# Written order on four engines, and attention and norms in one step per weight unit: a two-layer trunk on one Trainium2 core

## The chip, the core and the metric

The kernel runs on one core of one Trainium2 chip. The metric is device time in microseconds (us) of one execution; the median of three runs before the change is 2303.36 us (2301.89 to 2307.71). The profile comes from one further execution.

Five engines work side by side: PE (TensorE, matrix products), DVE (VectorE), ACT (ScalarE), POOL (GpSimd) and SP (SyncE, which only starts DMA transfers here). Each has a queue of its own and takes its instructions in the order in which they stand there; semaphores tell one engine when another's result is ready. An instruction that waits holds up all that stand behind it on its engine.

## The reference

256 rows of width 2048 go through two layers, all in float32. Cut to what matters:

```python
# layer 1
u = rms_norm(h, a_norm_g)
q, k, v, fz = split(u @ a_w_in)              # 3 x 2048 columns and 16 gate columns
q, k = rms_norm per head of 128 (a_q_g, a_k_g)
logf = log_sigmoid(fz + a_b_f)
o = softmax(q k^T / sqrt(128) + c_q - c_k, causal) v     # c = cumsum(logf); 16 heads
h = h + o @ a_w_out
h = h + relu(rms_norm(h) @ w1)**2 @ w2       # 2048 -> 8192 -> 2048
# shared keys and values, then layer 2
k, v = split(rms_norm(h, kv_norm_g) @ kv_w); k = rms_norm per head
q = rms_norm per head of (rms_norm(h, b_norm_g) @ b_w_q)
o = softmax(q k^T / sqrt(128) + bias_by_distance, causal by chunks of 64) v
h = h + o @ b_w_out
h = h + relu(rms_norm(h) @ w1)**2 @ w2
```

## The kernel before

**Precision.** Every weight and every activation is split into a rounded part and a rest (`hi`, `lo`), and a product is made of three: hi x hi, hi x lo, lo x hi (lines 305 to 307). The weight split is `issue` (lines 118 to 127): ACT copies the raw piece to `hi` (L125), DVE subtracts (L126).

**Weights.** They come in 768 pieces of 128 x 1024 floats (512 KB, one DMA on SP each, L115), in the order in which they are used. A piece holds two blocks of 128 rows by 512 columns. `fetch` keeps split pieces ready: before the products of piece n are written, the split of piece n+2 is written, and the loads of pieces up to n+5. There are three buffers for split pieces and four for raw ones. So the split of piece n+2 needs the buffer of piece n-1.

**Panels.** A panel is 512 output columns: eight pieces, each followed by 12 matmuls of 512 columns (two row blocks, two halves, three products) into an accumulator pair in PSUM, of which there are two. `panels` (L309) writes, for each piece: fetch, products, then `run_fill`; after the last piece it writes the evacuation. A "woven" stage runs its first two panels at once, piece by piece in turn, so that its input may arrive late; it takes both accumulator pairs.

**Fill.** `fill` is a list of lists of small work items; `run_fill` pops one list after each piece. `add_fill` lays items over the coming pieces. This is how the work between the products is spread: items at index 3 are written after the fourth next piece.

**Turning data.** The output of a panel has rows on the partitions, the next product wants columns there. DVE transposes blocks of 32 (`blocks32`, L176), then `carry` (L182) writes the tile to DRAM by one DMA (L189) and reads it back by four (L195), on SP. Fill lists of `carry`: store at index 0, reads at 2, use at 6.

**Layer 1 attention.** For each of four groups of four heads there is a q, a k and a v panel. `head_norm` (L328) evacuates q and k: ACT squares, DVE sums, POOL takes the power -0.5, DVE scales and transposes, all at the panel's end. `attend` (L399) lays one `softmax` per head on four consecutive pieces from index 6 on, and one `values` per head three pieces after the last. In the first panel `load_x` (L422) also loads the input (sixteen DMAs of 128 KB), scales and splits it and sums its squares by columns (`ColumnStats`, L225). `gates` (L442) makes the forget gates and `decay_bias` their logits. Then come the output projection with `next_x` (L203: add to h, sum squares, transpose, carry, split), four chunks of MLP, the q projection of layer 2, and its four groups of a k and a v panel.

**Order.** The program is written in this order, but a planner in the compiler sorts each engine's instructions by its own estimate of when their inputs will be ready, with the written place as priority. So an instruction can stand on its engine ahead of ones written before it.

Of the kernel before, what the change touches and what calls it, by code (L numbers as in the profile page):

```python
# [31 lines left out]
REL = 384  # L32


@with_exitstack
def trunk(ctx: ExitStack, tc: tile.TileContext, xT, xr, gs, hg, bf, wgate, w_in, w_oa, w1a, w2a,
          w_kv, w_qb, w_ob, w1b, w2b, rel, out):
    nc = tc.nc
    V, S, G, TE = nc.vector, nc.scalar, nc.gpsimd, nc.tensor
# [19 lines left out]
    x0 = wk.tile([P, T], F32, name="xin", tag="wk")  # L59
    nc.sync.dma_start(x0, xT[:, 0, :])  # L60
    gsb = const.tile([P, 5 * KT], F32, name="gsb")
    nc.sync.dma_start(gsb, gs)
# [46 lines left out]
    def load(parts=1):  # L109
        src = units.popleft()  # L110
        raw = wraw.tile([P, UN], F32, name="raw")
        n = UN // parts
        cuts = [slice(i * n, (i + 1) * n) for i in range(parts)]
        for c in cuts:
            nc.sync.dma_start(raw[:, c], src[:, c])  # L115
        raws.append((raw, cuts))
# [49 lines left out]
    def split_turned(t, n, which, into):  # L166
        x = acts.tile([P, 2, GH, T], F32R, name="act")
        y = qkv.tile([P, GH * T], F32, name="z").rearrange("p (k t) -> p k t", k=GH)
        for j in range(GH):
            m = which * KT + GH * n + j  # L170
            S.activation(y[:, j].rearrange("p (b i c) -> p b i c", b=NB, i=4), t[:, j], AF.Copy, scale=gsb[:, m : m + 1])  # L171
        S.activation(x[:, 0], y, AF.Copy)
        V.tensor_tensor(x[:, 1], y, x[:, 0].bitcast(F32), op=ALU.subtract)
        into.extend(x[:, :, j, :] for j in range(GH))

# [6 lines left out]
    def carry(z, dst):  # L182
# [4 lines left out]
        def rows():  # L187
            box.append(dram.tile([P, w], F32, name="turn", tag=f"turn{w}", bufs=4))
            nc.sync.dma_start(box[0], z)  # L189

        def columns():
            s = box[0].rearrange("(i a) f -> a i f", i=4)
            d = dst.rearrange("p (i f) -> p i f", i=4)
            for j in range(4):
                nc.sync.dma_start(d[32 * j : 32 * j + 32], s[:, :, j * n : (j + 1) * n])  # L195

        return [[rows], [], [columns], [], [], []]
# [5 lines left out]
    def next_x(n, r2, stats, which, into, kept=None):  # L203
# [3 lines left out]
        def use(flipped=False, which=which, into=into):  # L207
# [3 lines left out]
            split_turned(t, n, which, into)  # L211
# [12 lines left out]

    class ColumnStats:  # L225
        def __init__(self):
            self.acc = const.tile([P, T], F32, name="sqacc")
            self.n = 0

        def add(self, x):  # L230
            if self.n == 0:
                S.activation(self.acc, x, AF.Square)
            else:
                t = wk.tile([P, T], F32, name="sqt", tag="wk")
                S.activation(t, x, AF.Square)
                V.tensor_tensor(self.acc, self.acc, t, op=ALU.add)
            self.n += 1

        def reduce(self):
            pm = ps_o.tile([P, 512], F32, name="pt", tag="po")  # L240
            for b in range(NB):
                TE.matmul(pm[:, 2 * b : 2 * b + 2], self.acc[:, b * P : (b + 1) * P], ones[:, :2], start=True, stop=True)
            ms = sm.tile([P, NB], F32, name="ms")
            V.tensor_scalar(ms, pm[:, 0 : 2 * NB : 2], 1.0 / D, EPS, op0=ALU.mult, op1=ALU.add)
            self.r, self.e = root(ms, "a"), scaled(ms, "a")

        def spread(self):
            self.R = const.tile([P, T], F32, name="R")
            pr = ps_o.tile([P, 512], F32, name="pt", tag="po")
            for b in range(NB):  # L250
                rb = wk.tile([P, P], F32, name="rb", tag="wk")
                V.tensor_scalar(rb, ones[:, :P], self.r[:, b : b + 1], None, op0=ALU.mult)
                TE.matmul(pr[:, b * P : (b + 1) * P], rb, ident, start=True, stop=True)
            V.tensor_copy(self.R, pr[:, :T])
# [11 lines left out]
    class RowStats:  # L266
# [22 lines left out]

        def flip(self):  # L290
# [37 lines left out]
    def head_norm(e, z, dst):  # L328
        def f(b, ps):
# [5 lines left out]
            V.tensor_scalar(vv, ss, 1.0 / P, e[:, b : b + 1], op0=ALU.mult, op1=ALU.add)  # L335
# [3 lines left out]
            V.tensor_tensor(qn.rearrange("p (a d) -> p a d", a=GH), ps.rearrange("p (a d) -> p a d", a=GH),  # L339
                            rn.unsqueeze(2).to_broadcast([P, GH, P]), op=ALU.mult)  # L340
            blocks32(qn, z, b)
            if b == NB - 1:
                add_fill(carry(z, dst))
# [17 lines left out]
    def softmax(st, g, a, q, k, bias, cq):  # L361
        s = ps_s.tile([P, 512], F32, name="s")
        TE.matmul(s[:, 0:P], q[:, a, 0:P], k[:, a, 0], start=True, stop=True)
        TE.matmul(s[:, P : 3 * P], q[:, a, P:T], k[:, a], start=True, stop=True)
        t = wk.tile([P, 3 * P], F32, name="t", tag="wk")
# [4 lines left out]
        for b, c in ((0, slice(0, P)), (1, slice(P, 3 * P))):  # L370
# [5 lines left out]
            V.tensor_reduce(nm[:, b : b + 1], t[:, c], axis=AX.X, op=ALU.max, negate=True)  # L376
            S.activation(pr[:, c], t[:, c], AF.Exp, bias=nm[:, b : b + 1], accum_out=su[:, b : b + 1])  # L377
        V.reciprocal(rs, su)
        for b, c in ((0, slice(0, P)), (1, slice(P, 3 * P))):
            V.tensor_scalar(pr[:, c], pr[:, c], rs[:, b : b + 1], None, op0=ALU.mult)  # L380
        st["p"] = pr
        flip(st)

    def flip(st):
        z = prob.tile([P, 3 * P], F32, name="z", bufs=3)
        blocks32(st["p"], z, 0)
        st["pT"] = prob.tile([P, 3 * P], F32, name="prT")
        add_fill(carry(z, st["pT"]))
# [10 lines left out]
    def attend(g, q, k, v, bias, cq, o):  # L399
        st = [{} for _ in range(GH)]  # L400
        k4 = k.rearrange("p (i a b c) -> p a b i c", i=4, a=GH, b=NB)
# [17 lines left out]
    st0 = ColumnStats()  # L419
    x = []  # L420

    def load_x(u):  # L422
        for m in range(u * UA, (u + 1) * UA):
            xm = x0
            if m:
                xm = wk.tile([P, T], F32, name="xin", tag="wk")
                nc.sync.dma_start(xm, xT[:, m, :])
            x.append(split_x(xm, m, 0))
            st0.add(xm)
            if m in (0, UA):  # L430
                issue(2)
        if u == 1:
            nc.sync.dma_start(hgb, hg)
            nc.sync.dma_start(bfb, bf)
            V.tensor_scalar(gqk, hgb[:, 0:2], float(P) ** -0.5, None, op0=ALU.mult)
            V.tensor_tensor(gqk, gqk, hgb[:, 2:4], op=ALU.mult)
        if u == KT // UA - 1:
            st0.reduce()
# [3 lines left out]
    def gates(x, st):  # L442
        wgr = const.tile([P, KT * H], F32, name="wgr")
        nc.sync.dma_start(wgr, wgate)
# [19 lines left out]
        def logs():  # L464
# [8 lines left out]
            V.scalar_tensor_tensor(z, u, -1.0, u, op0=ALU.mult, op1=ALU.max)  # L473
            S.activation(z, z, AF.Exp, scale=-1.0)
            S.activation(z, z, AF.Ln, bias=1.0)
            V.scalar_tensor_tensor(z, u, 0.0, z, op0=ALU.min, op1=ALU.subtract)
            V.tensor_tensor_scan(c, ones[:H, :], z, 0.0, op0=ALU.mult, op1=ALU.add)
            nct = wk.tile([H, REL], F32, name="nct", tag="wk")
# [3 lines left out]
            nc.sync.dma_start(ct["cd"], nct)  # L482
# [8 lines left out]
        return [[lambda u=u: products(u)] for u in range(KT // UG)] + [[logs], [], [], [], [], [turn_c]]  # L491

    def decay_bias(g):
        nb = qkv.tile([P, GH, REL], F32, name="bias")
        src = ct["cd"][g * GH : (g + 1) * GH, :]
        nc.sync.dma_start(nb, src.unsqueeze(0).to_broadcast([P, GH, REL]))
        for c in (slice(0, P), slice(2 * P, 3 * P)):
            V.tensor_tensor(nb[:, :, c], nb[:, :, c], tri.unsqueeze(1).to_broadcast([P, GH, P]), op=ALU.add)
        return nb

    o = [None] * H
    for g in range(NG):
        zq, lq = turned("z")
        box = {}
        panels(x, [lambda b, ps: head_norm(st0.e, zq, lq)(b, ps)], load_x if g == 0 else None)
        add_fill([[]] * 6 + [[lambda box=box, lq=lq: box.update(q=scale_q(lq, 0))]])
        if g == 0:
            add_fill([[], [], [], [st0.spread]] + gates(x, st0))
        if g == 1:
            for b in range(NB):  # L510
# [3 lines left out]
        panels(x, [head_norm(st0.e, zk, k)])  # L514
        add_fill([[]] * (4 if g == 0 else 0) + [[lambda g=g, box=box: box.update(b=decay_bias(g))]])
        add_fill([[]] * (3 if g == 0 else 0) + attend(g, lambda box=box: box["q"], k, v, lambda box=box: box["b"], lambda: ct["cq"], o))
        panels(x, [v_evac(v, st0.r)])

    def mlp(x, st, last):
        for c in range(NCH):  # L520
            hid = []

            def take(t):
# [4 lines left out]
                S.activation(hi, t, AF.Square)  # L528
                S.activation(t, t, AF.Square)  # L529
                V.tensor_tensor(lo, t, hi.bitcast(F32), op=ALU.subtract)  # L530
                hid.extend(y[:, :, j, :] for j in range(GH))

            def turn_hidden():
                zt = []

                def f(b, ps):
# [3 lines left out]
                    if b == NB - 1:  # L540
                        add_fill(carry(*zt) + [[lambda: take(zt[1])]])
# [11 lines left out]
    add_fill([[], [st2.both], [st2.flip], []] + [[lambda n=n: kept[n](True, 2, xkv)] for n in range(NG)])  # L553
# [3 lines left out]
    for g in range(NG):  # L557
        box = {}

        def f(b, ps, box=box):  # L560
            if b == 0:
                z, lq = turned("z")
                box["f"] = head_norm(st2.e, z, lq)
                add_fill([[]] * 6 + [[lambda: qs.append(scale_q(lq, 1))]])
            box["f"](b, ps)
        evs.append(f)
# [3 lines left out]
    def rel_bias(g):  # L570
# [83 lines left out]
```

## Time and profile before

| what | value |
|---|---|
| median of three runs | 2303.36 us |
| the profiled execution's own time | 2303.8 us |
| its span, first to last instruction | 2301.7 us |
| mean granted TensorE clock | 0.978 |
| weight splits, L125 on ACT and L126 on DVE | 770 each, 1056 and 1218 ns |
| products, L305 to L307 | 3072 each |
| DMA | 491.60 MB, mean 214 GB/s |

The 40 slices of the span show where TensorE is busy and at which clock:

```profile
PE   7989989999999999999998988899999999999999
PEclk8999999999999999999999999999999999999999
DMA  5656666777667667667776755667775775776775
```

Each digit is a fortieth of the span, 57.5 us, in tenths of busy time, of full clock, or of the DMA engines. Layer 1's attention lies in slices 1 to 7, its MLP up to about slice 20, layer 2's attention around slices 22 to 27. A busy TensorE is not one at its peak, as the ends of its records are modelled; the number of matmuls in a window says more. The SP queue's waits, longest first, from its own view:

```profile
SPq L115 <- DVE lo L126: 1416.7, 624, 10.9
SPq L195 <- DMA turn<-z: 110.7, 58, 4.0
SPq L189 <- DVE z L179: 88.8, 63, 4.1
```

That is the line that waits, whom it waits for, the sum in us, how often, and the longest.

### The profile page before, as it was taken

The page shows a single profiled execution, that of the slowest core. Times are in us where ns is not written, and L with a number is a line of the kernel's source. Part 1 is how long each engine was busy: PE and PEld are TensorE (multiplying, and loading weights), DVE is VectorE, ACT ScalarE, POOL GpSimd, SP SyncE. Part 2 cuts the span into 40 slices and gives each one's busy share as a digit, 9 for nine tenths or more (in the row PEclk, how much of TensorE's full clock was granted, in tenths as well). Part 3 has the DMA queues.
Part 4 walks back from the last instruction along what each step waited for, and adds up shares of the span by engine and source line. Part 5 has one row for each costly group of instructions (what it writes and reads, how often), then busy time and mean ns, then how long its engine had stood idle before and what let it go on. Part 6 is the DMA issues. An engine that isn't in the chain of part 4 may idle for free. (4 is left out here: it accounts for less than half of the span.)

```text
span 2301.7 us, 25837 instructions
## 1 busy us (share of the span) xinstructions
PE 2199.6 (96%) x9518; PEld 1802.2 (78%) x9518; DVE 1267.9 (55%) x1478; ACT 1050.0 (46%) x1251; POOL 47.6 (2%) x48
## 2 busy tenths in 40 slices
PE   7989989999999999999998988899999999999999
PEld 4767777787888888888786877777788888888887
DVE  4666555555555555555565655565555555555554
ACT  4443433545345345345564533345543443443443
POOL 0100000000000000000001100000000000000000
PEclk8999999999999999999999999999999999999999
DMA  5656666777667667667776755667775775776775
GB/s 199 217 181 207 222 186 208 239 233 236 197 218 240 194 218 241 195 213 247 207 234 208 226 181 183 188 203 233 221 239 193 231 231 194 229 229 193 228 232 168
DMA packets 184174, 491.60 MB, mean 214 GB/s; under 512 B 36960, under 2 KB 76016, under 8 KB 183792
## 3 DMA queue, kind: packets, MB, share of 16 engines
q1 hardware_dynamic: 184048, 489.96, 67.4%
q8 instruction: 74, 1.21, 0.2%
q14 instruction: 52, 0.43, 0.1%
HBM read 450.01 MB, written 39.87 MB: 213 GB/s over the span
## 5 line engine op out<-in xcount | busy, mean ns | idle before, releaser
L126 DVE TENSOR_TENSOR lo<-raw,hi 128x1024 fp32r<-128x1024 f32 (+1 forms) x770 | 935.5, 1218 | 793.8 <-ACT hi L125 785.8
L125 ACT ACTIVATE hi<-raw 128x1024 fp32r<-128x1024 f32 (+1 forms) x770 | 811.0, 1056 | 990.2 <-PE acc L307 937.3
L305 PE MATMUL acc<-hi,act 128*128 128x512 f32 x3072 | 1216.8, 396 | 47.7 <-ACT hi L125 29.4
L306 PE MATMUL acc<-lo,act 128*128 128x512 f32 x3072 | 1216.5, 396 | 44.4 <-DVE lo L126 44.1
L307 PE MATMUL acc<-hi,act 128*128 128x512 f32 x3072 | 1211.7, 395 | 2.0 <-DVE act L163 1.9
L306 PEld LDWEIGHTS acc<-lo,act 128*128 128x128 f32 x3072 | 585.9, 191 | 177.6 <-DVE lo L126 56.6
L305 PEld LDWEIGHTS acc<-hi,act 128*128 128x128 f32 x3072 | 585.4, 191 | 177.8 <-ACT hi L125 34.9
L307 PEld LDWEIGHTS acc<-hi,act 128*128 128x128 f32 x3072 | 586.5, 191 | 126.3 <-DVE act L163 4.6
L396 ACT ACTIVATE act<-po 128x256 fp32r<-128x256 f32 x32 | 12.3, 384 | 117.5 <-PE po L394 117.5
L397 DVE TENSOR_TENSOR act<-po,act 128x256 fp32r<-128x256 f32 x32 | 13.5, 422 | 87.2 <-ACT act L396 87.2
L179 DVE STREAM_TRANSPOSE z<-acc 128x512 f32<-128x512 f32 x64 | 42.0, 695 | 20.7 <-PE acc L307 20.7
L337 POOL TENSOR_TENSOR rn<-vv,mhalf 128x4 f32<-128x4 f32 x32 | 42.0, 1312 | 440.3 <-DVE vv L335 440.3
L331 ACT ACTIVATE sq<-acc 128x512 f32<-128x512 f32 x32 | 19.0, 598 | 68.7 <-DVE qn L339 33.6
L377 ACT ACTIVATE pr<-t,nm 128x128 f32<-128x128 f32 x64 | 28.7, 449 | 26.3 <-DVE nm L376 25.7
L339 DVE TENSOR_TENSOR qn<-acc,rn 128x512 f32<-128x512 f32 x32 | 22.1, 691 | 32.4 <-POOL rn L337 32.4
L530 DVE TENSOR_TENSOR act<-q,act 128x1024 fp32r<-128x1024 f32 x32 | 39.0, 1218 | 0.0
L333 DVE TENSOR_REDUCE ss<-sq 128x4 f32<-128x512 f32 x32 | 21.6, 674 | 26.5 <-ACT sq L331 26.4
L528 ACT ACTIVATE act<-q 128x1024 fp32r<-128x1024 f32 x32 | 34.0, 1062 | 1.0
L524 ACT ACTIVATE q<-q 128x1024 f32<-128x1024 f32 x32 | 33.4, 1044 | 0.6 <-DMA q<-turn 0.6
L529 ACT ACTIVATE q<-q 128x1024 f32<-128x1024 f32 x32 | 33.3, 1042 | 0.0
L171 ACT ACTIVATE z<-q,gsb 128x256 f32<-128x256 f32 x64 | 27.4, 495 | 3.2 <-DMA q<-turn 2.2
L358 DVE SCALAR_TENSOR_TENSOR h<-acc,qn,h 128x512 f32<-128x512 f32 x32 | 22.6, 747 | 11.0 <-PE acc L307 11.0
(99 smaller groups left out, 432.6 us busy)
## 6 DMA issues: line engine op xcount, KB each, us to landing
raw<-in_w1a SPq DMA_DIRECT2D x128, 512.0 KB, 4.3
raw<-in_w2a SPq DMA_DIRECT2D x128, 512.0 KB, 4.3
raw<-in_w1b SPq DMA_DIRECT2D x128, 512.0 KB, 3.8
raw<-in_w2b SPq DMA_DIRECT2D x128, 512.0 KB, 3.6
raw<-in_w_in SPq DMA_DIRECT2D x94, 512.0 KB, 4.5
raw<-in_w_kv SPq DMA_DIRECT2D x64, 512.0 KB, 4.7
turn<-z SPq DMA_DIRECT2D x60, 512.0 KB, 4.1
q<-turn SPq DMA_DIRECT2D x176, 128.0 KB, 5.5
```

The source lines that it names most:

```text
L125: S.activation(hi[:, c], raw[:, c], AF.Copy)
L126: V.tensor_tensor(lo[:, c], raw[:, c], hi[:, c].bitcast(F32), op=ALU.subtract)
L179: V.transpose(z.rearrange("p (j n b c) -> p b n j c", j=4, n=n, b=nb)[:, b], src.rearrange("p (n j c) -> p n j c", n=n, j=4))
L305: TE.matmul(ps[b], xh, wh, start=k == 0, stop=False)
L306: TE.matmul(ps[b], xh, wl, start=False, stop=False)
L307: TE.matmul(ps[b], xl, wh, start=False, stop=k == KT - 1)
L337: G.tensor_tensor(rn, vv, mhalf, op=ALU.pow)
L377: S.activation(pr[:, c], t[:, c], AF.Exp, bias=nm[:, b : b + 1], accum_out=su[:, b : b + 1])
L524: S.activation(t, t, AF.Relu)
L528: S.activation(hi, t, AF.Square)
L529: S.activation(t, t, AF.Square)
L530: V.tensor_tensor(lo, t, hi.bitcast(F32), op=ALU.subtract)
```

## The change

1. **Order.** At the end of the program `keep_order` adds an ordering edge from each instruction on DVE, ACT, PE and SP to the one written before it on that engine. The planner can then no longer sort these four queues; POOL's is left free.
2. **Attention and norms in steps.** Work items become generators; each `yield` ends what is written after one piece. A head's softmax is four steps (scores; bias and maximum; exponential; normalise and transpose), heads start `GAP` = 3 pieces apart (2 in the last group of a layer), and values follow eight pieces after the scores were begun. `head_norm` keeps its sums at the panel's end, but the scaling and the transpose of each row block are laid on the next two pieces. `next_x` lays its transposes on the next piece, and starts its carry from there. Splits of turned inputs, the MLP's `take`, the gates' `logs`, and the biases are cut in two or three steps. `carry` waits one piece fewer before use, and for attention's probabilities one fewer between store and reads.
3. **Square sums from rows.** `ColumnStats` goes. The first norm's statistics come from `RowStats` on h, whose eight blocks of 256 KB are loaded in pieces 2 to 5 of the first panel and squared in pieces 4 to 7; before, h was loaded by two DMAs of 1 MB, written after the first group.
4. **Input in pairs.** x comes by eight DMAs of 256 KB, two pieces ahead; weight loads in the first panel keep fewer split pieces ready at first.

```diff
+def keep_order(tc, engines):
+
+    last = {}
+    for i in tc.nc.cur_bb.bb.instructions:
+        if i.engine in engines:
+            if i.engine in last:
+                tc.add_manual_dep(i, last[i.engine], mybir.DependencyInfo(mybir.DependencyClass.NoSync, mybir.DependencyReason.DATA),
+                                  reason="written order")
+            last[i.engine] = i.name
...
+    def steps(make):
+        box = []
+
+        def step():
+            if not box:
+                box.append(make())
+            next(box[0])
+        return step
...
-        return [[rows], [], [columns], [], [], []]
+        return [[rows]] + [[]] * wait + [[columns], [], []]
...
+        def turn():
+            zt.extend(turned(bufs=4))
+            for b in range(NB):
+                blocks32(h[b][:, n * 512 : (n + 1) * 512], zt[0], b)
+
         def f(b, ps):
             add_h(b, ps)
             stats.add(b, n)
-            if b == 0:
-                zt.extend(turned(bufs=4))
-            blocks32(h[b][:, n * 512 : (n + 1) * 512], zt[0], b)
             if b == NB - 1:
-                add_fill(carry(*zt) + [[use]])
+                step = steps(use)
+                add_fill([[turn], [lambda: add_fill(carry(*zt) + [[step], [step]])]])
...
-                hi, lo = fetch(min(u, AHEAD), min(u // 2, EARLY)) if before else fetch()
+                hi, lo = fetch(min(u // 2, AHEAD), 2) if before else fetch()
...
-            qn = wk.tile([P, 512], F32, name="qn", tag="wk")
-            V.tensor_tensor(qn.rearrange("p (a d) -> p a d", a=GH), ps.rearrange("p (a d) -> p a d", a=GH),
-                            rn.unsqueeze(2).to_broadcast([P, GH, P]), op=ALU.mult)
-            blocks32(qn, z, b)
+
+            def turn():
+                qn = wk.tile([P, 512], F32, name="qn", tag="wk")
+                V.tensor_tensor(qn.rearrange("p (a d) -> p a d", a=GH), ps.rearrange("p (a d) -> p a d", a=GH),
+                                rn.unsqueeze(2).to_broadcast([P, GH, P]), op=ALU.mult)
+                blocks32(qn, z, b)
+
+            rns.append(turn)
             if b == NB - 1:
-                add_fill(carry(z, dst))
+                add_fill([[t] for t in rns] + carry(z, dst))
...
-        A = [[lambda a=a: softmax(st[a], g, a, q(), k4, bias(), cq() if cq else None)] for a in range(GH)]
-        C = [[lambda a=a: values(st[a], a, v, o, g * GH + a)] for a in range(GH)]
-        return [[]] * 6 + A + [[]] * 3 + C
+        items = [[] for _ in range(15 + gap * GH)]
+        step = steps(lambda: make_bias(g, box))
+        items[1].append(step)
+        items[4].append(step)
+        items[5].append(step)
+        for a in range(GH):
+            at = 7 + gap * a
+            step = steps(lambda a=a: softmax(st[a], g, a, q(), k4, box["b"], cq() if cq else None))
+            for i in range(4):
+                items[at + i].append(step)
+            items[at + 3].append(lambda a=a: add_fill(st[a]["carry"]))
+            items[at + 8].append(lambda a=a: values(st[a], a, v, o, g * GH + a))
+        return items
...
+    def begin(u):
+        if u == 0:
+            load(2)
+            load_x(1)
+            load(2)
+        if u + 2 < KT // UA:
+            load_x(u + 2)
+        for j in range(UA):
+            x.append(split_x(raw_x[u][:, j], u * UA + j, 0))
...
+        if 2 <= u < 6:
+            for b, n in chunks[2 * u - 4 : 2 * u - 2]:
+                c = slice(n * 512, (n + 1) * 512)
+                SY.dma_start(h[b][:, c], xr[b][:, c])
+        if 4 <= u:
+            for b, n in chunks[2 * u - 8 : 2 * u - 6]:
+                st0.add(b, n)
...
-            add_fill([[], [], [], [st0.spread]] + gates(x, st0))
-        if g == 1:
-            for b in range(NB):
-                nc.sync.dma_start(h[b], xr[b])
+            add_fill([[st0.spread]] + gates(x, st0))
...
-    add_fill([[], [st2.both], [st2.flip], []] + [[lambda n=n: kept[n](True, 2, xkv)] for n in range(NG)])
+    again = [steps(lambda n=n: kept[n](True, 2, xkv)) for n in range(NG)]
+    add_fill([[], [st2.both], [], [st2.flip]] + [[]] * 6 + [[again[i // 2]] for i in range(2 * NG)])
...
     mlp(x3, st3, store)
+    keep_order(tc, (V.engine, S.engine, TE.engine, SY.engine))
```

More of the change, by code (lines that the diff above doesn't have):

```diff
@@ L114, in load @@
         for c in cuts:
-            nc.sync.dma_start(raw[:, c], src[:, c])
+            SY.dma_start(raw[:, c], src[:, c])
         raws.append((raw, cuts))
@@ L180, in blocks32, with carry @@
                     src.rearrange("p (n j c) -> p n j c", n=n, j=4))
-    def carry(z, dst):
+    def carry(z, dst, wait=1):
         w = z.shape[1]
@@ L210, in use @@
                 t = t[:, :, :, ::-1, ::-1]
-            split_turned(t, n, which, into)
+            return split_turned(t, n, which, into)
+        def turn():
+            zt.extend(turned(bufs=4))
+            for b in range(NB):
+                blocks32(h[b][:, n * 512 : (n + 1) * 512], zt[0], b)
         def f(b, ps):
@@ L223, in next_x @@
         return f
[L225 to L240, printed above, removed]
-            for b in range(NB):
[L242 to L254, printed above, removed]
     def root(ms, name):
@@ L288, in both, with roots, spread @@
             self.e = scaled(self.ms, self.name)
+        def roots(self):
+            self.both()
+            self.r = root(self.ms, self.name)
+        def spread(self):
+            self.R = const.tile([P, T], F32, name="R")
+            pr = ps_o.tile([P, 512], F32, name="pt", tag="po")
+            for b in range(NB):
+                rb = wk.tile([P, P], F32, name="rb", tag="wk")
+                V.tensor_scalar(rb, ones[:, :P], self.r[:, b : b + 1], None, op0=ALU.mult)
+                TE.matmul(pr[:, b * P : (b + 1) * P], rb, ident, start=True, stop=True)
+            V.tensor_copy(self.R, pr[:, :T])
         def flip(self):
@@ L326, in stage, with head_norm @@
             panels(x, [e])
-    def head_norm(e, z, dst):
+    def head_norm(stats, z, dst):
+        rns = []
         def f(b, ps):
@@ L369, in softmax @@
         rs = sm.tile([P, NB], F32, name="rs")
-        for b, c in ((0, slice(0, P)), (1, slice(P, 3 * P))):
+        halves = ((0, slice(0, P)), (1, slice(P, 3 * P)))
+        for b, c in halves:
             if cq is not None:
@@ L416, in add_fill @@
                 fill.append(it)
-    st0 = ColumnStats()
+    st0 = RowStats("x")
     x = []
[L422 to L431, printed above, removed]
+    chunks = [(b, n) for n in range(NG) for b in range(NB)]
+    def begin(u):
[7 more added lines that the diff above has]
+            x.append(split_x(raw_x[u][:, j], u * UA + j, 0))
         if u == 1:
-            nc.sync.dma_start(hgb, hg)
-            nc.sync.dma_start(bfb, bf)
+            SY.dma_start(hgb, hg)
+            SY.dma_start(bfb, bf)
             V.tensor_scalar(gqk, hgb[:, 0:2], float(P) ** -0.5, None, op0=ALU.mult)
             V.tensor_tensor(gqk, gqk, hgb[:, 2:4], op=ALU.mult)
+        if 2 <= u < 6:
[5 more added lines that the diff above has]
+                st0.add(b, n)
         if u == KT // UA - 1:
-            st0.reduce()
+            st0.roots()
     ct = {}
@@ L481, in logs @@
             ct["cd"] = dram.tile([H, REL], F32, name="cd")
[L482 removed]
+            SY.dma_start(ct["cd"], nct)
+            yield
         def turn_c():
@@ L489, in turn_c, with decay_bias @@
             V.tensor_copy(ct["cq"].rearrange("p b h -> p (b h)"), pc[:, : NB * H])
-        return [[lambda u=u: products(u)] for u in range(KT // UG)] + [[logs], [], [], [], [], [turn_c]]
-    def decay_bias(g):
+        step = steps(logs)
+        return ([[lambda: SY.dma_start(wgr, wgate)], []] + [[lambda u=u: products(u)] for u in range(KT // UG)]
+                + [[step], [step], [step], [], [turn_c]])
+    def decay_bias(g, box):
         nb = qkv.tile([P, GH, REL], F32, name="bias")
         src = ct["cd"][g * GH : (g + 1) * GH, :]
[L496 to L499, printed above, removed]
+        SY.dma_start(nb, src.unsqueeze(0).to_broadcast([P, GH, REL]))
+        yield
+        V.tensor_tensor(nb[:, :, :P], nb[:, :, :P], tri.unsqueeze(1).to_broadcast([P, GH, P]), op=ALU.add)
+        yield
+        c = slice(2 * P, 3 * P)
+        V.tensor_tensor(nb[:, :, c], nb[:, :, c], tri.unsqueeze(1).to_broadcast([P, GH, P]), op=ALU.add)
+        box["b"] = nb
+        yield
     o = [None] * H
@@ L540, in f @@
                     if b == NB - 1:
-                        add_fill(carry(*zt) + [[lambda: take(zt[1])]])
+                        step = steps(lambda: take(zt[1]))
+                        add_fill(carry(*zt) + [[step], [step]])
                 return f
@@ L581, in trunk @@
         v = qkv.tile([P, NB, 512], F32, name="v")
-        panels(xkv, [head_norm(st2f.e, zk, k)])
-        box = {}
-        box["b"] = rel_bias(g)
-        add_fill(attend(g, lambda g=g: qs[g], k, v, lambda box=box: box["b"], None, o))
-        panels(xkv, [v_evac(v, st2f.r)])
+        panels(xkv, [head_norm(lambda: st2.flipped, zk, k)])
+        add_fill(attend(g, lambda g=g: qs[g], k, v, None, o, rel_bias, GAP if g < NG - 1 else 2))
+        panels(xkv, [v_evac(v, st2.flipped.r)])
     st3, x3 = RowStats("n"), []
```

71 lines of the change are left out of this document (43 added, 28 removed).

## The prediction

> **What bounds the kernel now.** I read the page first, then the waits of TensorE, then busy time by stage, then the timeline around one wait.
>
> ```profile
> PE 2199.6 (96%) x9518; PEld 1802.2 (78%) x9518; DVE 1267.9 (55%) x1478; ACT 1050.0 (46%) x1251; POOL 47.6 (2%) x48
> ```
> ```profile
> engine line waited for: us in total, times, longest us
> PE acc L306 <- DVE lo L126: 44.1, 29, 3.6
> PE acc L305 <- ACT hi L125: 29.4, 20, 2.7
> PE acc L305 <- ACT act L162: 11.7, 6, 2.9
> PE acc L305 <- DVE qn L339: 6.4, 1, 6.4
> ```
> TensorE is the bound. DVE and ACT are half idle, yet TensorE waits about 96 us for them, nearly always for a weight split (`hi`, `lo`).
>
> ```profile
> 5.50:54.40 48.90, 33.70 (x97) 22.15 (x97) 21.38 (x41) 19.99 (x38) 0.00 (x0) 0.79 0.61 211
> 54.40:107.70 53.30, 51.33 (x220) 40.96 (x220) 35.12 (x56) 24.09 (x32) 8.55 (x7) 0.97 0.62 201
> 107.70:415.80 308.10, 278.78 (x1185) 225.55 (x1184) 178.93 (x293) 127.91 (x196) 16.89 (x14) 0.96 0.65 204
> 415.80:464.70 48.90, 45.43 (x193) 37.08 (x192) 28.52 (x29) 26.91 (x39) 0.00 (x0) 0.97 0.76 235
> 464.70:1120.10 655.40, 653.11 (x2881) 540.48 (x2881) 352.34 (x323) 305.12 (x301) 0.00 (x0) 1.00 0.69 220
> ...
> 1168.80:1268.00 99.20, 90.37 (x388) 73.73 (x388) 60.46 (x70) 53.61 (x70) 8.61 (x7) 0.97 0.68 212
> 1268.00:1548.60 280.60, 255.30 (x1089) 207.97 (x1088) 159.45 (x270) 116.62 (x183) 12.46 (x12) 0.95 0.63 195
> ```
> The columns are window, its length, busy time of PE, PEld, DVE, ACT and POOL, granted clock, DMA share and GB/s. I call the 12 products of one 128x1024 weight piece a unit; there are 768. The fifth row (240 units, one wait of 2.3) gives the pace: 653.1 / 240 = 2.72 us a unit. Against it: first panel 48.9 - 8 x 2.72 = **27.1 over**. Layer 1's attention to the middle of its output projection (third row, 88 units): 239.4, plus 32 score and value steps of four matmuls at 0.72 us (23.0), leaves **45.7 over**, of which the waits in that window are 29.4. Layer 2's (last row, 80 units): 217.6 + 23.0, **40.0 over**, waits 25.3. So 54.7 us of waits drag 31.0 us of slow clock behind them: 0.57 us for each us waited.
>
> ```profile
> 145.93 0.38 ACT L396 ACTIVATE act<-po 128x256 fp32r<-128x256 f32 x1 [5.22 <-PE po L394]
> 146.22 1.05 ACT L125 ACTIVATE hi<-raw 128x1024 fp32r<-128x1024 f32 x1
> 146.35 0.42 DVE L397 TENSOR_TENSOR act<-po,act 128x256 fp32r<-128x256 f32 x1 [3.96 <-ACT act L396]
> 147.30 1.22 DVE L126 TENSOR_TENSOR lo<-raw,hi 128x1024 fp32r<-128x1024 f32 x1 [0.52 <-ACT hi L125]
> 147.32 0.49 PE L305 MATMUL acc<-hi,act 128*128 128x512 f32 x1 [1.42 <-ACT hi L125]
> ...
> 148.57 0.79 PE L306 MATMUL acc<-lo,act 128*128 128x512 f32 x1 [0.76 <-DVE lo L126]
> ```
> This is the mechanism. ACT stood 5.22 us before a copy that needed this unit's value product, with the next weight split queued behind it. The planner had put L396 ahead of L125, so TensorE waited 1.42 for `hi`, 0.76 for `lo`, and then ran at 0.79 us a matmul record.
>
> [...]
>
> **The change, part by part.** Everything below is in us.
>
> *Written order.* Now `hi` and `lo` of unit n+2 stand on ACT and DVE ahead of the fill items of unit n. They may start when TensorE ends unit n-1, so they have two units, 5.44, for 1.06 + 1.22: TensorE feels nothing until DVE or ACT is 3.16 late. DVE has 2.72 - 1.22 = 1.50 spare a unit, ACT 2.72 - 1.06 = 1.66; a unit with a score or value step gives 0.72 more.
>
> *Attention in steps.* Per head: scores; a unit later DVE adds bias and reduces (0.34 + 0.47 + 0.27 + 0.41 = 1.49); then ACT exp (0.40 + 0.50 + 2 x 0.19 = 1.28); then DVE reciprocal, scaling and transpose (0.16 + 0.28 + 0.35 + 0.57 = 1.36); value step five units on (DVE 0.42). Heads follow three units apart. Head norm leaves 1.8 at a panel's end and moves 0.69 + 0.71 = 1.40 into each of two later units. The worst units, counted from the V panel, are 15 (1.8 + 0.42), 16 (1.36 + 1.40) and 17 (1.49 + 1.40). Backlog after each: 2.22 - 2.22 = 0; 2.76 - 2.22 = 0.54; 0.54 + 2.89 - 1.50 = 1.93; in unit 18 it is gone. 1.93 is under 3.16. Layer 2, sixteen units a group, meets the same sum. The last group's heads two units apart reach 1.35. Each step's input was made a unit earlier, so nothing waits on its neighbour. A transpose issues one row DMA and four column DMAs on SP: rows land in 4.1 (192 KB: 2.5), columns in 5.5; they have 2 (heads: 1) and about 3 units. A load of unit n+5 is needed three units, 8.2, later and lands in 4.5, so SP can stand 3.7 without harm. The cover for all these zeros is that two-unit lead; without it each DVE step costs its 1.4. I leave one 0.76 wait (the `lo` row above) in each of eight groups, with slow clock 8 x 0.76 x 1.57 = 9.5. Bounds: 0, and half of the present overrun, 43. **Gain 85.7 - 9.5 = 76.2.**
>
> *First panel.* x comes in eight 256 KB pairs two units ahead; square sums move to rows of h, whose eight 256 KB loads now stand on SP between x and weights in units 2 to 5. To the last input of the panel SP asks for 8 x 0.26 + 8 x 0.26 + 8 x 0.52 MB = 8.3 MB. The 10 to 25 us windows moved 338 to 371 GB/s: 25 us. So DMA isn't last; ACT is: units 5 to 7 need two splits (0.50), two squares with sums (0.62 + 0.19) and `hi`, 3.68 against 2.72, and unit 4 a second `hi`, 4.74: 3 x 0.96 + 2.0 = 4.9. In unit 1 DVE stands in `gqk` for `hgb` (twelfth on SP, at 0.43 an issue near 5.5; 4.1 to land, behind 2.6 MB), ahead of `lo`: PE idle about 2.7. Together 7.6 x 1.57 = 11.9 over. Bounds: 6, and 22 if DMA stays at this window's 211 GB/s. The dropped column sums (15 DVE adds of 0.42) lay beside idle DVE. **Gain 27.1 - 11.9 = 15.2.**
>
> *Spread and gates.* Written order puts the spread matmuls between units 8 and 9, while their DVE input stands behind both head-norm sums, a `lo` and the first moved step: 2.4 + 1.2 + 1.4 + 0.3 = 5.3 after unit 7, 2.6 late. Each of two gate products waits for POOL's memset (which needs a buffer that the preceding unit frees), ACT and DVE: 0.95 + 0.31 + 0.29 and handover = 1.75, with TensorE standing. 6.1 x 1.57 = 9.6, where the second row above has 53.3 - 43.5 - 4.5 (gate and spread matmuls) = 5.3. **Loss 4.3** (0 to 10).
>
> *Stage seams.* At the end of the first layer's output projection, third panel, DVE ran residual, transposes, then `lo`: 48.9 - 43.5 = 5.4 over; so at three places, 16. Now two residual panels' splits and squares meet in units 22 to 24: `hi` of unit 26 stands behind 3.0 of splits and 1.6 of squares and lets TensorE wait 0.5, `lo` of unit 27 behind a split and the transposes 1.9; 2.4 x 1.57 x 3 = 11.3. **Gain 4.7.** The wait of 2.3 after each first w1 stage goes (DVE has `lo` ahead of the transposes): **gain 4.6.** In layer 2's query stage (99.2 - 87.1 = 12.1 over) the third panel wants the accumulator that the second moved norm step still reads. That step stands behind the kv split, the first step, the second panel's sums and a `lo`: 1.2 + 1.4 + 1.8 + 1.2 + 1.4, and some 1.6 of waiting in front, so TensorE idles about 8.6, x 1.57 = 13.5. **Loss 1.4** (bounds: gain 6, loss 8).
>
> *Sum:* 76.2 + 15.2 - 4.3 + 4.7 + 4.6 - 1.4 = 95.0. The profiled run took 2303.8 with a span of 2301.7; the median is 2303.4, so the same difference is taken from it: **2208**. The MLP units (512 of 768) gain nothing else.
>
> **Rivals.** (a) *All waits go*, the clock never drops in the attention stages, and seams vanish: 2303.4 - 85.7 - 18 - 20 - 5 = 2175. For it: 1.93 against 3.16. Against: DMA landings spread (4.3 median, 10.0 longest for transposes). (b) *Half stays*: columns land late, TensorE now stands in a score or value step where the planner had put it later. 2208 + 43 - 9.5 = 2242. For: k lands about a unit ahead of its first use. Against: values come five units after their weights. (c) *The weight queue becomes the bound*, and the kernel slower. SP in written order holds weight loads behind column DMAs that wait for rows. Once the stand exceeds 3.7 each us reaches TensorE; with 56 transposes in the attention stages it eats the gain from 3.7 + 95 / (56 x 1.57) = 4.8 us a transpose. At 5.5 (the columns' landing) it costs 56 x 1.8 x 1.57 = 158: 2366. For: SP stood 110.7 in 58 such waits. Against: 35.5 of them fell in the 655 us of MLP where TensorE waited 2.3 in all. (d) *The order isn't kept*: the planner still sorts, only the first panel gains: 2288 to 2305, about 2295. (e) *The clock holds through short waits*: the 0.57 parts of my sums fall away, 3.4 + 4.3 + 3.5 + 4.1 + 4.9 = 20.2, so 2188. Against: the 0.79 row above. [...]
>
> **How the numbers follow.** Forecast 0.57, by itself 2185 to 2235; (e) 0.05; (a) 0.10; (b) 0.14; (d) 0.04; (c) 0.10. 0.3% is 7 us, what a measurement of this kernel can tell. Faster: the forecast, (e), (a), (b) and half of (d), 0.88; same 0.02; slower 0.10. The range 2175 to 2260 holds the forecast, (e), most of (b) and a third of (a), about 0.78.
>
> **What would show it.** L396 and L397 after the next L125 and L126; TensorE waits in the attention stages down from 54.7 to some 6; a first panel of 31 to 37 us; short waits at the spread and gate products; one wait near 8 in layer 2's query stage; MLP windows at clock 1.00 and 2.72 a unit. Wrong would be: weight loads as releasers of L125, or many waits of TensorE before L363 or L393.

## The result, and the profile after

The changed kernel takes 2199.97 us (median of four runs, 2196.73 to 2203.54) against 2305.53 (median of four) for the kernel before: ratio 0.9542, 95% interval 0.9519 to 0.9566. Its profiled execution took 2199.56 us with a span of 2197.8. The span is 103.9 us shorter. The page's line on busy time, share and count of each engine:

```profile
PE 2160.6 (98%) x9514; PEld 1781.1 (81%) x9514; DVE 1274.4 (58%) x1464; ACT 1049.1 (48%) x1251; POOL 48.3 (2%) x48
```

The waits of TensorE after the change (line that waits, whom for, sum in us, how often, longest). L142 and L143 are the weight splits, formerly L125 and L126; L319 to L321 are the products.

```profile
PE acc L320 <- DVE lo L143: 7.7, 11, 2.2
PE acc L319 <- DVE qn L357: 7.4, 1, 7.4
PE acc L319 <- ACT hi L142: 7.2, 7, 2.0
PE s L499 <- DVE hi L496: 3.5, 2, 1.7
PE pt L301 <- DVE rb L300: 3.3, 1, 3.3
```

The two waits for weight splits fell from 73.5 to 14.9 us. What is new stands in the last two lines: the gate products (L499) and the spread (L301). By stage, with the columns of the windows shown before (length, PE, PEld, DVE, ACT, POOL, clock, DMA share, GB/s):

```profile
6.60:35.20 28.60, 24.96 (x96) 18.72 (x97) 18.41 (x31) 20.64 (x41) 0.71 (x1) 1.00 0.95 344
35.20:94.20 59.00, 52.23 (x218) 41.96 (x217) 33.85 (x50) 23.23 (x29) 6.65 (x6) 0.94 0.60 194
94.20:356.00 261.80, 261.40 (x1183) 216.77 (x1182) 181.62 (x287) 127.48 (x196) 16.25 (x12) 1.00 0.72 234
...
1108.60:1205.50 96.90, 89.21 (x387) 73.15 (x386) 61.56 (x71) 55.72 (x73) 8.80 (x7) 0.96 0.68 216
1205.50:1445.10 239.60, 239.60 (x1090) 199.28 (x1090) 163.67 (x269) 114.97 (x183) 14.77 (x14) 1.00 0.74 233
```

The third and the last row are the attention stages: clock 1.00, TensorE busy throughout. One wait of 0.4 us is left there, for a probability tile that a DMA brings; it was 54.7. The second row is the place that became worse, at clock 0.94. The table cuts both kernels at the same products. "Over" is what a stage takes beyond 2.72 us for each of its units; the gain is the difference of the stages' times.

| stage | over, before | over, after | gain | forecast |
|---|---|---|---|---|
| first panel (gain includes its start, at 5.5, then 6.6) | 27.1 | 6.9 | 19.1 | 15.2 |
| spread and gates (next two panels) | 9.8 | 15.5 | -5.7 | -4.3 |
| two attention stages, with 46 us of matmuls of their own | 131.7 | 44.2 | 87.5 | 76.2 |
| three residual seams | 16.0 | 19.4 | -3.4 | 4.7 |
| after the first w1 stage of each layer | 5.2 | 1.0 | 4.2 | 4.6 |
| layer 2's query stage | 12.1 | 9.9 | 2.2 | -1.4 |
| sum | | | 103.9 | 95.0 |

A value step of the same group of heads as in the prediction's timeline, now on ACT:

```profile
145.78 0.39 ACT L418 ACTIVATE act<-po 128x256 fp32r<-128x256 f32 x1 [1.34 <-PE po L416]
146.06 1.05 ACT L142 ACTIVATE hi<-raw 128x1024 fp32r<-128x1024 f32 x1
```

In the prediction's timeline ACT stood 5.22 us ahead of such a copy, with a split behind it that TensorE needed next. Now it stands 1.34, and the split behind it isn't needed for two units.

### The profile page after: what moved, and what is told of

Same layout as the page of the kernel before. It is cut to its first block, busy times and chain, and to the rows that moved or that the text cites. A ratio compares the mean times of both kernels' runs of the same rounds, so it can differ in the third digit from the quotient of the medians.

```text
span 2197.8 us, 25786 instructions
## 1 busy us (share of the span) xinstructions
PE 2160.6 (98%) x9514; PEld 1781.1 (81%) x9514; DVE 1274.4 (58%) x1464; ACT 1049.1 (48%) x1251; POOL 48.3 (2%) x48
## 4 chain that ended last, share of the span: by engine, by line
PE 91%; DMA 3%; ACT 2%; DVE 2%; issue 1%; SPq 0%; POOL 0%; DVEq 0%; ACTq 0%; POOLq 0%
PE acc L320 30%; PE acc L321 30%; PE acc L319 30%; DMA raw<-in_w_in 1%; ACT hi L142 1%; DMA turn<-z 1%; DVE lo L143 1%; PE po L415 1%; PE s L384 1%; DMA raw<-in_w_ob 0%; DMA raw<-in_w_oa 0%; ACT act L191 0%; DMA raw<-in_w2a 0%; ACT z L188 0%; PE po L416 0%
## 5 line engine op out<-in xcount | busy, mean ns | idle before, releaser
L143 DVE TENSOR_TENSOR lo<-raw,hi 128x1024 fp32r<-128x1024 f32 (+1 forms) x770 | 936.7, 1218 | 810.5 <-ACT hi L142 802.9
L142 ACT ACTIVATE hi<-raw 128x1024 fp32r<-128x1024 f32 (+1 forms) x770 | 811.7, 1057 | 1002.9 <-PE acc L321 960.5
L319 PE MATMUL acc<-hi,act 128*128 128x512 f32 x3072 | 1210.1, 394 | 15.3 <-DVE qn L357 7.4
L320 PE MATMUL acc<-lo,act 128*128 128x512 f32 x3072 | 1201.1, 391 | 7.7 <-DVE lo L143 7.7
L321 PE MATMUL acc<-hi,act 128*128 128x512 f32 x3072 | 1199.7, 391 | 0.8 <-DVE act L180 0.8
L319 PEld LDWEIGHTS acc<-hi,act 128*128 128x128 f32 x3072 | 579.3, 189 | 137.8 <-ACT hi L142 10.0
L320 PEld LDWEIGHTS acc<-lo,act 128*128 128x128 f32 x3072 | 579.3, 189 | 133.1 <-DVE lo L143 14.5
L321 PEld LDWEIGHTS acc<-hi,act 128*128 128x128 f32 x3072 | 578.8, 188 | 122.6 <-DVE act L180 2.0
L274 ACT ACTIVATE sqr<-h 128x512 f32<-128x512 f32 x32 | 19.9, 624 | 22.3 <-DVE h L376 14.0
L349 DVE TENSOR_REDUCE ss<-sq 128x4 f32<-128x512 f32 x32 | 21.8, 681 | 14.2 <-ACT sq L347 14.2
L192 DVE TENSOR_TENSOR act<-z,act 128x1024 fp32r<-128x1024 f32 x16 | 19.6, 1226 | 10.4 <-ACT act L191 10.4
```

Source lines behind the costliest of these rows:

```text
L142: S.activation(hi[:, c], raw[:, c], AF.Copy)
L143: V.tensor_tensor(lo[:, c], raw[:, c], hi[:, c].bitcast(F32), op=ALU.subtract)
L319: TE.matmul(ps[b], xh, wh, start=k == 0, stop=False)
L320: TE.matmul(ps[b], xh, wl, start=False, stop=False)
L321: TE.matmul(ps[b], xl, wh, start=False, stop=k == KT - 1)
```

## The experiments

Three kernels' worth of change stand in one diff: an order, smaller items, another start. The first runs take the order apart.

**The steps without any order.**

```diff
-    keep_order(tc, (V.engine, S.engine, TE.engine, SY.engine))
```

> The changed kernel without its written order: the planner sorts all queues again, steps and front as changed. Theory (the order took the waits away, the steps only make an order possible that has no long item in it): the planner again puts copies that need a fresh score or value product ahead of weight splits; TensorE waits in the two attention stages for L142/L143 stay at 25 to 50 us (after: 0.4; before: 54.7), time 2235 to 2290. Rival (the small steps alone do it): waits under 5, time 2195 to 2212.

2217.48 us, ratio 0.9607 (0.9579 to 0.9634): neither range. The steps and the new start alone bring 88 of the 106 us. By the spans, 56 us of this lie in the attention stages and 23 in the first panel and its start. In the two attention stages TensorE waits 19 us, 9.0 and 10.0 (here and below, waits of over 0.25 us are added up). The first two rows of its waits over the whole run:

```profile
PE acc L320 <- DVE lo L143: 20.7, 22, 2.3
PE acc L319 <- ACT hi L142: 11.2, 12, 1.9
```

**The order without the steps**, on the kernel before.

```diff
     mlp(x3, st3, store)
+    keep_order(tc, (nc.vector.engine, nc.scalar.engine, nc.tensor.engine, nc.sync.engine))
```

> The kernel before, with the written order on DVE, ACT, PE and SP and nothing else of the change. Theory (order without steps moves the wait): a head's softmax is then one item on four units in a row, DVE 1.49 + 1.36 plus about 0.7 of standing for ACT's exponential, against 1.50 spare, so about 1.3 to 2 late a head, 3.16 of lead per group: some 6 us of waits in each of 8 groups, 48 against 54.7 before; time 2265 to 2320. Rival (the order alone does it): waits under 10, time 2200 to 2230.

2310.34 us, ratio 1.0017 (1.0001 to 1.0032), in the theory's range. Its attention waits are 58.5, where the theory had 48; its first panel is 14 us better than before, and its spread and gates 15 worse.

```profile
PE acc L317 <- DVE lo L137: 77.5, 43, 4.3
PE acc L316 <- ACT hi L136: 8.2, 15, 1.5
```

Where the planner let TensorE wait for ACT and DVE, the written order with a whole head in one item lets it wait for DVE. So in written order the long items alone are enough to keep the time, and with the new items the planner's order costs only what is left of the waits.

**The order on DVE and ACT alone, and on PE and SP alone**, with the steps.

```diff
-    keep_order(tc, (V.engine, S.engine, TE.engine, SY.engine))
+    keep_order(tc, (V.engine, S.engine))
```

> The changed kernel with the order kept on DVE and ACT only. Theory (what stood in the way was a weight split behind a waiting instruction on ACT or DVE): as the changed kernel, 2195 to 2212, attention waits under 4. Rival (TensorE's or SP's own order matters too: products and weight loads behind late ones): attention waits over 10, time over 2220.

> The changed kernel with the order kept on PE and SP only. Theory: ACT and DVE are sorted again, so as the run with no order at all, 2235 to 2290, waits for L142 and L143. Rival (the queue of SP or PE made the difference): 2195 to 2215.

Both theories fell. DVE and ACT alone: 2216.67 (0.9603, 0.9575 to 0.9631), as with no order at all, with 18.6 of attention waits. PE and SP alone: 2193.71 (0.9504, 0.9475 to 0.9532), with 3.7. The timeline of ACT, and TensorE's next product, in the kernel with only DVE and ACT in order say why:

```profile
134.18 1.06 ACT L142 ACTIVATE hi<-raw 128x1024 fp32r<-128x1024 f32 x1
141.92 0.38 ACT L418 ACTIVATE act<-po 128x256 fp32r<-128x256 f32 x1 [6.68 <-PE po L416]
142.20 2.94 ACT L142 ACTIVATE hi<-raw 128x1024 fp32r<-128x1024 f32 x3
...
143.30 0.50 PE L319 MATMUL acc<-hi,act 128*128 128x512 f32 x1 [1.42 <-ACT hi L142]
```

The copy stands in its written place, and ACT still waits 6.68 us before it, because the value product itself comes late on TensorE. That product (L415) is written after the first 41 units. The kernel here has it 24 products, two units, later; the one with no order 31. With no order 13 of the 32 value steps stand at the end of a unit; with PE in order all 32 do, where they were written. The two units that the planner put in front use up the splits that were ready. The split of the next unit stands behind the copy, and TensorE waits 1.42 us for it.

**PE alone, SP alone.**

```diff
+    keep_order(tc, (TE.engine,))
```

> The changed kernel with the order kept on PE alone. New theory (after the run with DVE and ACT alone changed nothing): what made a weight split late was a score or value product that the planner put several products too late on TensorE; the copy that needs it then holds ACT and DVE. So PE's order alone does what PE and SP did together: 2188 to 2200, attention waits under 8. Rival (SP's order brings weights and transposes in time): 2212 to 2222.

> The changed kernel with the order kept on SP alone. New theory: TensorE's products are sorted again, so as with no order, 2212 to 2222, waits for L142 and L143 of 25 to 35 in all. Rival (SP's order is what counts): 2188 to 2200.

PE alone: 2192.76 (0.9505, 0.9468 to 0.9543), with 5.5 of attention waits; the theory holds. SP alone: 2230.35 (0.9668, 0.9627 to 0.9710), outside both ranges, with 27.8 of waits. That is 13 us more than with no order at all, though the intervals of the two ratios still touch. So of the four queues TensorE's gives the whole gain of the order. Kept on all four, the spans are 6.5 to 7.1 us longer than on PE, or on PE and SP; the intervals of the ratios overlap, so that this isn't shown by the times. The stages show a place for it: at the three residual seams 19.4 over with all four, 5.2 with PE alone.

**PE and SP in order on the old items.**

> The kernel before, whole-head items, with the order kept on PE and SP. If the place of the products on TensorE is what matters and the steps only help, the attention waits of 54.7 fall by more than half: 2230 to 2275. If the long items are themselves the larger part (a head's DVE work with ACT in its middle, between two splits), the waits stay over 40: 2285 to 2320. The run with all four orders on the old items (2310) speaks for the second.

2304.56 (0.9998, 0.9987 to 1.0010); attention waits 42.9: the second of the two expectations. TensorE's order pays only once the items are short.

**One unit of lead, not two.**

```diff
-AHEAD = 2
+AHEAD = 1
```

> The changed kernel with weight splits one unit ahead and not two (AHEAD = 1); all else as changed. Theory (the lead of two units is the cover of the steps): a lead of one leaves 2.72 - 2.28 = 0.44 of slack, single steps of 1.4 to 1.5 still fit the 1.50 spare, but a panel's end with a head norm (2.4 of chain before the next lo) and the two units where a head's step and a norm's step meet overshoot: some 4 us a group in 8 groups, and more at the seams and where MLP steps of 2.1 meet on ACT, so 30 to 70 us of waits more and 2240 to 2310. Rival (steps fit between splits by themselves, lead not needed): 2200 to 2212.

2239.8 (0.9709, 0.9671 to 0.9748), at the lower edge of the range. The attention waits go from 0.4 to 14.2, the seams' from 10.8 to 18.3, and all of TensorE's from 32 to 58, so 26 more and not 30 to 70. The lead is a cover, worth 40 us.

**Which steps?** A head's four steps written after one unit, heads still three units apart; and the norm's scaling back at the panel's end.

```diff
-                items[at + i].append(step)
+                items[at].append(step)
```

> The changed kernel, all four orders kept, with a head's four steps written after one unit (heads still three units apart, everything else as changed). Theory (a step may be late by up to the 3.16 of lead; what counts is the standing inside an item): DVE stands for the scores, does 1.49, stands for ACT's exponential about 0.9, does 1.36, so it is about 0.7 + 1.5 + 0.9 + 1.4 - 1.2 = 3.3 to 4 behind at its worst against 3.16, and one unit with a norm step on top is over it: 0.3 to 1 a head and 2 more a group, 20 to 35 of waits in the 8 groups, time 2225 to 2260. Rival (spacing the heads three units apart is enough): waits under 6, time 2198 to 2212.

```diff
-                add_fill([[t] for t in rns] + carry(z, dst))
+                for t in rns:
+                    t()
+                add_fill([[], []] + carry(z, dst))
```

> The changed kernel, all four orders kept, with head_norm's scaling and transposes at the panel's end and not on the next two units. Theory: the next split stands behind the chain square 0.6, sum 0.7, 0.2, POOL 1.3, scale and transpose 1.4, and the second block's 1.4: ready at about 6.9 after the panel's end against 5.44 of lead, 1.5 late in each of 16 panels with a head norm, less in layer 2's query stage, where the accumulator is free sooner (7.4 falls to about 2): 24 - 5 = 19 of waits more, with slow clock up to 30: 2212 to 2232. Rival (only the heads' work was too long): 2185 to 2203.

The whole head costs nothing that the times show: 2200.56 (0.9538, 0.9510 to 0.9566), 1.3 us of attention waits. The theory fell: with heads three units apart and the norm in steps, cutting each head in four isn't needed here. The norm at once: 2224.58 (0.9642, 0.9614 to 0.9670), in the range, with 13.6 of attention waits. The part that I had wrong in it is the query stage: 10.4 of waits there, where I had expected its 7.4 to fall to about 2.

**Mending what still waits.** The gate weights get other buffers (those of the attention biases, still free), cleared at the start, and are split a unit before their products; the spread is three items; residual splits come later; the first query panel's norm is scaled at once; `gqk` comes two units later.

```diff
+PAD = (3, 4, 2, 0)
...
+                wg.append(qkv.tile([P, GH * REL], F32R, name="wg", tag="bias"))
+                G.memset(wg[-1][:, :UN].bitcast(F32), 0.0)
...
-        return ([[lambda: SY.dma_start(wgr, wgate)], []] + [[lambda u=u: products(u)] for u in range(KT // UG)]
+        return ([[lambda: SY.dma_start(wgr, wgate)], [], [lambda: prepare(0)],
+                 [lambda: products(0), lambda: prepare(1)], [lambda: products(1)]]
...
-                add_fill([[turn], [lambda: add_fill(carry(*zt) + [[step], [step]])]])
+                add_fill([[turn], [lambda: add_fill(carry(*zt) + [[]] * PAD[n] + [[step], [step]])]])
...
-                box["lq"], box["f"] = lq, head_norm(lambda: st2, z, lq)
+                box["lq"], box["f"] = lq, head_norm(lambda: st2, z, lq, g == 0)
```

> The changed kernel, all four orders kept, with what still waits mended by place alone: gate weights cleared early in buffers of their own and split a unit ahead of their products; the spread in three steps; the splits of residual panels 0 to 2 laid 3, 4 and 2 units later; in layer 2's query stage the first panel's norm scaled at once and not two units on; gqk two units later. Theory (each of these waits is a placed instruction that stands in the way): gates and spread 6.8 of wait and 5.1 of slow clock go, seams 10.8 + 6.2 fall to a third, the query stage's 7.4 + 6.1 to about 4, unit 1's 2.2 goes: 2200 - 11.9 - 11 - 9 - 2 = 2166, range 2158 to 2178. Rival (the places are bound by DMA or by the sum of work on DVE, the waits turn up elsewhere): 2185 to 2203.

2172.76 us (2170.65 to 2173.80), ratio 0.9418 (0.9404 to 0.9432): the fastest of all. The largest of its waits:

```profile
PE acc L325 <- DVE lo L144: 4.8, 7, 0.8
PE acc L324 <- ACT hi L143: 2.3, 4, 1.1
PE acc L324 <- ACT sq L352: 2.2, 1, 2.2
```

Spread and gates went from 15.5 to 5.8 over (4.5 are their matmuls), the query stage from 9.9 to 4.4, the seams from 19.4 to 8.6. No line of the gates is left, and 0.6 of the spread.

> The same mends without the later residual splits, with the order kept on PE and SP alone (planner free on DVE and ACT, 2194 unmended). Theory: gates and spread 5.4 of wait and 3.0 of slow clock go, the query stage's 6.1 + 2 to about 4, so 2194 - 8 - 4 = 2182, range 2174 to 2190. Rival (the planner moves the DVE work into the way again): 2190 to 2200.

2182.16 us (2181.20 to 2184.03), 0.9462 (0.9446 to 0.9478), as expected by the theory. With DVE and ACT free the planner does the seams better (4.4 over) and the query stage and layer 1's attention worse (7.4; 28.1 against 22.3). In this kernel, once the places are mended by hand, all four orders are the better choice.

## Why the prediction was right, and where it wasn't

**The sum.** 2208 was forecast, 2199.97 measured; 95.0 of gain against 103.9. The largest term, attention, was 76.2 against 87.5. The 9.5 us left there for one missed `lo` a group didn't occur: 0.4 us of waits in both stages, and that one for a DMA.

But the backlog arithmetic (1.93 against 3.16) was too hopeful, and that no wait came of it was luck. In six of the eight groups one `lo` is ready only as TensorE comes to it, 0.06 to 0.12 us ahead of the product; the median in the two stages is 3.4 and 3.5 us ahead. The first of the six (unit 36, counted from 0):

```profile
129.51 1.18 DVE L143 TENSOR_TENSOR lo<-raw,hi 128x1024 fp32r<-128x1024 f32 x1
...
130.75 0.50 PE L320 MATMUL acc<-lo,act 128*128 128x512 f32 x1
```

So the lead was used up and not left with 1.2 to spare. The sum counted DVE's own work and not what it stands for: it waited 1.47 us for a value step's copy at 118.8 and 0.93 for ACT's squares at 120.2. That these two make up the rest is argued, not shown. The norm at once, which lays 2.8 at a panel's end, has 13.6 us of waits.

**The cause given for that term was partly wrong.** I took the ACT order, L396 ahead of L125, for the mechanism. With the new items and DVE and ACT in order, the time is that of no order; with the old items and all four queues in order, 58.5 us of attention waits are left, where there were 54.7. What failed in that step is the place of the fault: with the new items the copy waited because TensorE's own queue had the value product too late. In the prediction's own timeline, too, the product stood one unit behind its written place, after 36 units and not 35. I read who waited (ACT) and not where on TensorE the awaited product stood. The price of rival (d), the order isn't kept, fell with it: 2295, with a gain in the first panel alone, where that kernel takes 2217. The new items give most of the gain under the planner too, and TensorE's order alone 25 us more.

**First panel.** It took 28.6 us, less than the 31 to 37 named as a sign. The rate was as taken: 344 GB/s in that window, in the range of 338 to 371. Between its first product and its last TensorE waited 3.6 in place of 7.6: the `gqk` stand 2.2 (2.7 forecast), and 1.4 for splits of x, where ACT's surplus had been put at 4.9. Its first unit took 4.5 us, so 1.8 of the 6.9 over lie there. Of the 1.4 most came from DMA, which the sum didn't hold to be last. The weights of unit 6 took 7.5 us to land, ACT stood for them, and the splits of x that TensorE needed next stood behind:

```profile
23.82 1.06 ACT L142 ACTIVATE hi<-raw 128x1024 fp32r<-128x1024 f32 x1 [2.49 <-DMA raw<-in_w_in]
```

**Spread and gates.** 3.3 and 2 x 1.74 us were measured for 2.6 and 2 x 1.75. The gate wait can be read step by step, as it was summed:

```profile
53.20 0.95 POOL L492 MEMSET hi<- 128x1024 f32 x1 [13.75 <-PE acc L321]
54.19 0.31 ACT L495 ACTIVATE hi<-wgr 128x128 fp32r<-128x128 f32 x1 [2.67 <-POOL hi L492]
54.53 0.29 DVE L496 TENSOR_TENSOR hi<-wgr,hi 128x128 fp32r<-128x128 f32 x1 [1.75 <-ACT hi L495]
...
54.88 0.96 PE L499 MATMUL s<-act,hi 128*128 128x512 f32 x3 [1.74 <-DVE hi L496]
```

Mended, spread and gates gave back 9.7 us, so the mechanism is shown.

**Seams.** The waits were 3.3, 3.4 and 4.1 in place of 2.4 each, so that a gain of 4.7 became a loss of 3.4. In the first layer's projection (units counted from its first, as 0) `hi` of unit 26 did stand behind splits and squares, but it cost 1.50 and not 0.5, and its `lo`, made after it, 0.76 more. Unit 27, put at 1.9, had no wait. Unit 18, soon after the first two panels, had 0.31 and 0.76, which the sum put at nothing. The sum also left out where the long wait begins. Followed back in the profile's chain, it begins at all three seams with a weight load that took 8.2 to 9.7 us to land, where 4.5 had been taken. In layer 1:

```profile
379.31 1.06 ACT L142 ACTIVATE hi<-raw 128x1024 fp32r<-128x1024 f32 x1 [1.38 <-DMA raw<-in_w_oa]
```

The splits, the residual and the squares follow on this one, and then `hi` of unit 26. Laying the splits later took more than half of the loss back.

**Query stage.** One wait of 7.4 us at the accumulator, where I had 8.6. Scaling the first panel's norm at once brought it to 2.2.

**Rivals.** (b), half stays: one DMA in all was late for a value step, by 0.4, in layer 1. (c), the weight queue: SP stood 107.8 us in 53 waits for rows, 2.0 each, under the 4.8 that this rival needs. No weight load releases TensorE itself. On ACT weight loads do release L142, named as a sign of being wrong: 18.2 us in 14 waits. Before the change it was 22.1 in 16, and only in the first panel and at the seams does such a wait reach TensorE. (a) wasn't reached by this kernel; the mended one, at 2173, is where it was priced, 2175.

**What stays open.** What each part of the new items is worth, the spacing of the heads above all, wasn't tried by itself: only the head in one item (nothing) and the norm at once (25 us) were. Why SP alone in order takes longer than no order, and why the weight loads at the seams land so late, wasn't tried further. Nor was it tried to free DVE and ACT at the seams alone.

## What to carry to other kernels

When a copy waits long for a product, look at where that product stands on its own engine, against where it was written, before blaming the copy's queue. Lay the work so that the backlog on each engine, unit by unit, stays under the lead with which its results are made, and count in it what the engine stands for others; then keep the written order, on the engine that bounds the kernel first, and mend the few places where written order itself puts a fresh product in front of the next step. The order alone gave nothing here while the items were long; the new items and the new start without it gave most of the gain.

## What the runs showed of the hardware

The clock didn't fall after every short wait. After waits of 0.31 and 0.76 us it stayed at 1.00, and after 1.50 and 0.76 it fell to 0.69 (window, its length, busy times, clock, DMA share, GB/s):

```profile
363.90:370.00 6.10, 6.10 (x28) 5.01 (x27) 4.07 (x5) 2.12 (x2) 0.00 (x0) 1.00 0.92 298
...
388.50:394.00 5.50, 5.50 (x18) 4.25 (x18) 5.41 (x6) 2.78 (x3) 0.00 (x0) 0.69 0.55 130
...
13.70:19.20 5.50, 5.50 (x24) 4.57 (x25) 5.38 (x8) 3.93 (x7) 0.00 (x0) 1.00 0.97 308
```

Between the two waits of the second pair there is one matmul record of 0.50, so 2.26 us of idle time within 2.8 us stand ahead of the 0.69. Rival (e), 2188, would need a clock that holds through such waits, and the second row has one that doesn't. The third row follows the single wait of 2.20 at `gqk`, and its clock stayed at 1.00, while the 1.42 and 0.76 of the prediction's timeline, 2.18 in sum, were followed by a record of 0.79. So the sum of idle time alone doesn't decide it; what does wasn't tried.
